# Values of two head groups made by a Strassen scheme in one early stage

## The chip, the cores and the metric

The kernel runs on one core of a Trainium2 chip. The metric is the device time of one execution in microseconds (us). The engines are TensorE (PE; its weight loads are shown as PEld), VectorE (DVE), ScalarE (ACT), GpSimd (POOL) and SyncE (SP), whose queue issues most of the DMAs. A time is compared by the median of several runs; the profile is one execution more.

## The reference

One layer of a decoder trunk on 1024 tokens of width 1024, in float32. What matters here is the first half:

```python
h = rms_norm(x, pre_mix_g[l])
proj = h @ w_in[l]
qa, ka, va, qb, kb, vb, gates = jnp.split(proj, split_at, axis=-1)
qb = apply_rope(qb.reshape(b, s, B_GROUPS, B_HEADS, B_HEAD_DIM), cos_b, sin_b)
vb = vb.reshape(b, s, B_GROUPS, B_HEADS, B_HEAD_DIM)
for g, (window, dil) in enumerate(B_PAIRS):
    o_g, lse_g = dilated_group(qb[:, :, g], kb[:, :, g], vb[:, :, g], window, dil)
```

The first attention (A) is differential attention over 4 heads. The second (B) has three groups of 4 heads of 128 columns, with dilations 1, 4 and 16. The values `vb` of groups 1 and 2 are together `h` (1024 x 1024) times 1024 columns of `w_in`. Gates, a mixing product and a convolutional MLP follow.

## The kernel before

Every float32 product is made of two parts: `split` (L140, L143) makes a high part on ACT and the remainder on DVE, and three matmuls (`mm3`, L146 to L149) take high x high, low x high and high x low. x stands transposed as `xh` and `xl`, 8 slices k of 128 rows by 1024 tokens.

*Start.* Three gates are projected first, from weights in `first`, while x arrives slice by slice (`load_x`, `split_x`; L342 and L343 split it). Their six PSUM banks are copied out (L375, L376) and stored to `gt_d` (L377). Then x is read again by rows, squared on ACT (L383) and made into `rstd`, the inverse root; `tables` computes sine and cosine of the positions on DVE (L295 to L304) and ACT (L305, L306); they are scaled by `rstd`, which is turned into a row by transposes (L394), written to `tab_d` and read back by `load_tabs`. Two more gates, the first head of A and its values follow.

*A.* Each of its heads runs eight query blocks; `interleave` mixes pieces of other projections (fills) between them, by `yield`ed sizes.

*B.* It has 12 steps (pair of heads, group, head). Each step runs four jobs of `attend_b`, with the next step's `proj_b` as filler: 96 matmuls of 512 columns. Further filler are the values of the next group, by `proj_v` (L429 to L464): each call makes 256 columns for two heads, as 8 row blocks x 8 k x 3 matmuls of 256 columns (L438 to L440), half of them in each of two steps. For group 0 they are split at once (L448, L449). For groups 1 and 2 ACT scales them by `rstd` (L453), they are stored to `v_d`, loaded back in the dilated order as `vperm` (L463) and split there. Only the step (pair 1, group 2, first head) has no other filler than the projection of q and k; the last step has gates.

*What sets the order.* The kernel's text gives each instruction a priority, earlier first, and `tc.high_priority` moves some ahead; a planner with costs of its own then orders each engine's instructions when the kernel is built, and takes one that is ready before one of higher priority that isn't. Each engine and each DMA queue then works strictly in that order. Tiles with the same tag share buffers; a tile in a reused buffer waits until the earlier one has no reader left. PSUM has eight banks: three `acc`, two `pt`, two `s`, one `o`. Weights go through six pairs of buffers `wh`, `wl`, raw data through `raw`.

## Time and profile before

| | |
|---|---|
| median of 3 runs | 1754.89 us (1754.01 to 1755.79) |
| the profiled execution | 1754.33 us |
| its span | 1752.5 us |
| mean granted PE clock | 0.994 |
| PE / PEld / DVE / ACT busy | 98% / 84% / 74% / 50% |
| matmuls and transposes | 8942 |

A row of groups shows line, engine, operation, tiles, shape, count, busy time and mean duration in ns, then the idle time before them and who ended it. A row of windows shows start and end, length, and for PE, PEld, DVE, ACT and POOL the busy time and the count, then the granted PE clock, the share of the DMA engines and GB/s. A row of the timeline shows start, duration, engine, line and tiles. A row of waits shows who waited for whom, the total, how often, and the longest. A row of DMA issues shows the count, the size of one and the median time to landing.

### The profile page before, as it was taken

How to read it: one execution, taken by the hardware profiler on the slowest of the kernel's cores; microseconds unless marked ns; L12 is line 12 of the kernel's file. 1: busy time of each engine (PE TensorE's matmuls, PEld its weight loads, DVE VectorE, ACT ScalarE, POOL GpSimd, SP SyncE). 2: the span in 40 equal slices, each digit the busy share in tenths (PEclk: the TensorE clock that was granted, in tenths of full speed). 3: DMA queues.
4: the chain of work that ended last, by engine and by line, in shares of the span. 5: the costliest groups of instructions: out<-in, count | busy, mean ns of one | idle time of the engine just before them, and what ended most of it. 6: DMA issues, size and time to landing. Idle time of an engine off the chain costs nothing.

```text
span 1752.5 us, 24382 instructions
## 1 busy us (share of the span) xinstructions
PE 1724.8 (98%) x8942; PEld 1469.5 (84%) x8942; DVE 1295.2 (74%) x2548; ACT 868.1 (50%) x1585; POOL 50.5 (3%) x78
## 2 busy tenths in 40 slices
PE   9999999999999999999999999999999999999997
PEld 7888898889988888888887888878888888878886
DVE  4766877775455566554575767899998999689978
ACT  5456564643455645465662533364444444355452
POOL 0000000000000000000000400300000000000000
PEclk9999999999999999999999999999999999999998
DMA  7510112211131234231386542123222223196624
GB/s 262 186 55 31 65 57 73 85 49 55 55 97 55 97 98 154 72 96 55 117 293 207 161 152 97 36 76 99 91 85 90 78 74 105 55 340 215 209 78 156
DMA packets 100407, 197.62 MB, mean 113 GB/s; under 512 B 16368, under 2 KB 23216, under 8 KB 100288
## 3 DMA queue, kind: packets, MB, share of 16 engines
q1 hardware_dynamic: 92192, 185.06, 32.0%
q10 hardware_dynamic: 8096, 11.01, 1.7%
q8 instruction: 70, 1.15, 0.3%
q14 instruction: 49, 0.40, 0.1%
HBM read 152.37 MB, written 43.66 MB: 112 GB/s over the span
## 4 chain that ended last, share of the span: by engine, by line
PE 77%; DVE 8%; DMA 8%; ACT 3%; issue 3%; SPq 1%; POOL 0%; DVEq 0%; ACTq 0%; POOLq 0%
PE acc L147 15%; PE acc L148 15%; PE acc L149 15%; PE acc L438 3%; PE acc L440 3%; PE acc L439 3%; PE acc L1312 2%; PE acc L1313 2%; PE acc L1311 2%; PE o L485 2%; PE pt L472 2%; PE acc L989 2%; PE acc L990 2%; PE acc L988 2%; DVE wlo L140 1%
## 5 line engine op out<-in xcount | busy, mean ns | idle before, releaser
L147 PE MATMUL acc<-xh,whi 128*128 128x512 f32 x744 | 297.3, 401 | 3.9 <-ACT xh L342 2.5
L148 PE MATMUL acc<-xh,wlo 128*128 128x512 f32 x744 | 298.2, 401 | 1.5 <-DVE wlo L140 1.5
L149 PE MATMUL acc<-xl,whi 128*128 128x512 f32 x744 | 294.7, 398 | 0.0
L143 ACT ACTIVATE whi<-raw 128x512 fp32r<-128x512 f32 (+1 forms) x258 | 158.7, 624 | 206.3 <-PE acc L149 138.5
L140 DVE TENSOR_TENSOR wlo<-raw,whi 128x512 fp32r<-128x512 f32 (+1 forms) x255 | 180.5, 716 | 57.2 <-ACT whi L143 56.4
L147 PEld LDWEIGHTS acc<-xh,whi 128*128 128x128 f32 x744 | 140.5, 189 | 34.5 <-ACT xh L342 3.7
L148 PEld LDWEIGHTS acc<-xh,wlo 128*128 128x128 f32 x744 | 140.6, 189 | 29.0 <-DVE wlo L140 1.7
L149 PEld LDWEIGHTS acc<-xl,whi 128*128 128x128 f32 x744 | 140.8, 189 | 27.5
L147 PE MATMUL acc<-mh,whi 128*128 128x512 f32 x400 | 155.7, 390 | 0.3 <-ACT mh L143 0.2
L148 PE MATMUL acc<-mh,wlo 128*128 128x512 f32 x400 | 155.6, 389 | 0.0
L149 PE MATMUL acc<-ml,whi 128*128 128x512 f32 x400 | 155.4, 389 | 0.0
L438 PE MATMUL acc<-whi,xh 128*128 128x256 f32 x512 | 147.6, 288 | 1.0 <-DVE t L421 1.0
L440 PE MATMUL acc<-wlo,xh 128*128 128x256 f32 x512 | 148.1, 289 | 0.0
L439 PE MATMUL acc<-whi,xl 128*128 128x256 f32 x512 | 147.9, 289 | 0.0
L420 ACT ACTIVATE t<-acc 64x512 f32<-64x512 f32 (+1 forms) x160 | 94.7, 592 | 39.4 <-PE acc L149 36.9
L1186 DVE TENSOR_TENSOR u<-acc,u 128x512 f32<-128x512 f32 x133 | 90.6, 685 | 26.7 <-PE acc L149 26.7
L143 ACT ACTIVATE whi<-s 128x512 fp32r<-128x512 f32 x76 | 47.0, 628 | 106.9 <-PE acc L149 97.7
L438 PEld LDWEIGHTS acc<-whi,xh 128*128 128x128 f32 x512 | 97.7, 191 | 2.0 <-DVE t L421 1.4
L439 PEld LDWEIGHTS acc<-whi,xl 128*128 128x128 f32 x512 | 97.7, 191 | 0.6
L440 PEld LDWEIGHTS acc<-wlo,xh 128*128 128x128 f32 x512 | 97.7, 191 | 0.2
L147 PEld LDWEIGHTS acc<-mh,whi 128*128 128x128 f32 x400 | 75.1, 188 | 16.3 <-ACT mh L143 0.5
L149 PEld LDWEIGHTS acc<-ml,whi 128*128 128x128 f32 x400 | 75.1, 188 | 15.7
(311 smaller groups left out, 3875.6 us busy)
## 6 DMA issues: line engine op xcount, KB each, us to landing
raw<-in_w_in SPq DMA_DIRECT2D x126, 256.0 KB, 2.8
raw<-in_w_up SPq DMA_DIRECT2D x88, 256.0 KB, 2.8
raw<-c_d SPq DMA_DIRECT2D x48, 256.0 KB, 3.6
c_d<-c SPq DMA_DIRECT2D x22, 512.0 KB, 2.6
raw<-in_w_down SPq DMA_DIRECT2D x37, 256.0 KB, 4.0
gl<-gt_d SPq DMA_DIRECT2D x16, 512.0 KB, 5.2
gt_d<-gate ACTq DMA_DIRECT2D x26, 256.0 KB, 2.1
og_d<-osb SPq DMA_DIRECT2D x12, 512.0 KB, 3.0
```

What stands on the lines that cost most here:

```text
L140: eng.tensor_tensor(lo, src, hi.bitcast(F32), op=ALU.subtract)
L143: nc.scalar.activation(hi, src, AF.Copy)
L147: nc.tensor.matmul(o, sh, mh, start=first, stop=False)
L148: nc.tensor.matmul(o, sl, mh, start=False, stop=False)
L149: nc.tensor.matmul(o, sh, ml, start=False, stop=last)
L420: nc.scalar.activation(t1[dst], ps[src], AF.Copy)
L438: nc.tensor.matmul(ps, xh[:, k, tk], wh[:, w], start=k == 0, stop=False)
L439: nc.tensor.matmul(ps, xl[:, k, tk], wh[:, w], start=False, stop=False)
L440: nc.tensor.matmul(ps, xh[:, k, tk], wl[:, w], start=False, stop=k == KC - 1)
L472: nc.tensor.transpose(ps[:, n * P : (n + 1) * P], t, ident)
L485: nc.tensor.matmul(o[:, q0 : q1 + 1], vs[b // 4][0][:, b % 4, c], t[:, part], start=first and n == part == 0, stop=False)
L1186: nc.vector.tensor_tensor(to, made(p), x, op=ALU.add)
```

## The change

The four calls of `proj_v` for groups 1 and 2 go away. In their place, right after the first three gates, one stage makes all 1024 columns at once: x and the weights are cut into 2 x 2 blocks (512 x 512 each), and seven products of blocks give the result instead of eight (Strassen's scheme in Winograd's form, the one that the MLP of this kernel has too). `sums_x` makes three of the four sums of x while x arrives, and the fourth, negated, is written over block b12 of x itself before the loop; p7's steps load that block again. A step `n` is one product and one of its four k: `fetch_v` loads weights up to 8 steps ahead, `ready_v` sums and splits them up to 5 ahead, four groups of three matmuls follow, and after the fourth k `take_v` adds the four banks into `ys_v`. Two sets of four banks alternate between the products. At step 4 the squares of x are put in, at step 18 the angles, at step 26 the first two blocks of the result are scaled and stored by ACT's queue; the tables and their reloading stand behind the stage. `values_by` is what is left of `values_of` for groups 1 and 2: loads in dilated order and a split. The first gates take the slices of x in the order 0, 4, 1, 5, 2, 6, 3, 7, and x has six buffers instead of three.

```diff
+XT_BUFS, NORM_AT, ANGLES_AT, STORE_AT = 6, 4, 18, 26
+
+K_FIRST = (0, 4, 1, 5, 2, 6, 3, 7)
...
-            order += [("v", VB + g * 512 + pair * 256, i) for i in range(2)]
+            if g == 0:
+                order += [(VB + pair * 256, i) for i in range(2)]
...
-    v_d = dram.tile([4, S, 256], F32, name="v_d")
+    v_d = dram.tile([S, 1024], F32, name="v_d")
...
+    xw0 = open_pool(st_v, "xw0", side="right")
+    t2, t3, t4 = ([xw0.tile([P, 4, 512], F32R, tag=n + p, name=n + p) for p in "hl"] for n in ("t2", "t3", "t4"))
+    tb = open_pool(st_v, "tb", side="right")
+    kq, tq = [slice(i * 4, (i + 1) * 4) for i in range(2)], halves()
+    b11, b12, b21, b22 = ([t[:, k, t_] for t in (xh, xl)] for k in kq for t_ in tq)
...
         def load_x(k, parts=1):
-            xts[k] = prep.tile([P, S], F32, tag="xt", name="xt", bufs=3)
+            xts[k] = prep.tile([P, S], F32, tag="xt", name="xt", bufs=XT_BUFS)
...
+        t1_raw = [tb.tile([P, 2, 512], F32, tag=t, name="t1") for t in ("kk", "ang")]
+
+        def sums_x(k):
+
+            low, high = xts[k], xts[k + 4]
+            g1, g2 = gpre[:, k : k + 1], gpre[:, k + 4 : k + 5]
+            e, o = (tb.tile([P, 2, 512], F32, tag=t, name=t) for t in ("sin", "cos"))
+            nt1 = t1_raw[k // 2][:, k % 2]
+
+            def plus(out, x, g, y, op):
+                nc.vector.scalar_tensor_tensor(out, x, g, y, op0=ALU.mult, op1=op)
+
+            nc.scalar.activation(e[:, 0], low[:, 512:], AF.Copy, scale=g1)
+            plus(nt1, low[:, :512], g1, e[:, 0], ALU.subtract)
+            plus(e[:, 1], high[:, 512:], g2, e[:, 0], ALU.subtract)
+            split(t3[0][:, k], t3[1][:, k], e[:, 1])
+            plus(o[:, 0], high[:, 512:], g2, nt1, ALU.add)
+            split(t2[0][:, k], t2[1][:, k], o[:, 0])
+            plus(o[:, 1], high[:, :512], g2, o[:, 0], ALU.subtract)
+            split(t4[0][:, k], t4[1][:, k], o[:, 1])
...
-        load_x(1)
-        split_x(1)
+        load_x(4)
+        split_x(4)
         load_first(256, 1024)
         split_first(256, 512)
         split_first(512, 1024)
-        for k in range(2, KC):
+        for n, k in enumerate(K_FIRST[2:], 2):
             load_x(k)
             split_x(k)
+            if n % 2:
+                sums_x(K_FIRST[n - 3])
+        sums_x(3)
...
-        for k in range(KC):
-            w = slice(k * P, (k + 1) * P)
+        for j, k in enumerate(K_FIRST):
+            w = slice(j * P, (j + 1) * P)
             for n, ps in enumerate(pss):
                 (wh, wl), sl = first[n // 2], halves()[n % 2]
-                mm3(ps, wh[:, w], wl[:, w], xh[:, k, sl], xl[:, k, sl], k == 0, k == KC - 1)
+                mm3(ps, wh[:, w], wl[:, w], xh[:, k, sl], xl[:, k, sl], j == 0, j == KC - 1)
         for n, i in enumerate(FIRST_GATES):
...
-        for m in range(8):
-            t = prep.tile([P, D], F32, tag="xt", name="xn", bufs=3)
-            dma(t, a["x"][m * P : (m + 1) * P, :])
-            sq = prep.tile([P, D], F32, tag="kk", name="sq")
-            nc.scalar.activation(sq, t, AF.Square, accum_out=ssx[:, m : m + 1])
-        with tc.high_priority(offset=60):
-            nc.vector.tensor_copy(rstd, rsqrt(ssx, D, prep, "rx"))
-            spread = rstd_row.rearrange("p (m q) -> p m q", q=P)
-            nc.vector.tensor_copy(spread, rstd.unsqueeze(2).to_broadcast([P, 8, P]))
...
+    def norm_x():
+
+        ssx = tiny.tile([P, 2, 32], F32, name="ssx", bufs=1)[:, :, :8]
+        for m in range(8):
+            for half, sl in enumerate(halves()):
+                t = load_raw(a["x"][m * P : (m + 1) * P, sl], next(tags))
+                nc.scalar.activation(t, t, AF.Square, accum_out=ssx[:, half, m : m + 1])
+        tt(ssx[:, 0], ssx[:, 0], ssx[:, 1], ALU.add)
+        nc.vector.tensor_copy(rstd, rsqrt(ssx[:, 0], D, tb, "rx"))
+
+    def make_tables(*tab):
+        nc.scalar.activation(tab[0], tab[0], AF.Sin)
+        nc.scalar.activation(tab[1], tab[1], AF.Sin, bias=half_pi)
+        spread = rstd_row.rearrange("p (m q) -> p m q", q=P)
+        nc.vector.tensor_copy(spread, rstd.unsqueeze(2).to_broadcast([P, 8, P]))
+        neg = tb.tile([P, S], F32, tag="kk", name="neg")
+        for half, sl in enumerate(halves()):
+            row = psum(F32, pt, "pt")
+            for b in range(4):
+                nc.tensor.transpose(row[:, b * P : (b + 1) * P], spread[:, half * 4 + b], ident)
+            nc.scalar.activation(rstd_row[:, sl], row, AF.Copy)
+            nc.vector.scalar_tensor_tensor(neg[:, sl], tab[0][:, sl], -1.0, row, op0=ALU.mult, op1=ALU.mult)
+            nc.vector.tensor_tensor(tab[0][:, sl], tab[0][:, sl], row, op=ALU.mult)
+            nc.vector.tensor_tensor(tab[1][:, sl], tab[1][:, sl], row, op=ALU.mult)
+        for t, to in zip((tab[1], tab[0], neg), tab_d):
+            dma(to, t)
...
+    with ExitStack() as st_y:
+        wv = open_pool(st_y, "wv")
+        yv = open_pool(st_y, "yv")
+        order_v = (("p1", b11), ("p5", b12), ("p6", t2), ("p7", t3), ("p3", b22), ("p2", b21), ("p4", t4))
+        steps_v = [(p, x, k) for p, x in order_v for k in range(4)]
+        wa, wz = ([t[:, k % 2] for t in [q.tile([P, 2, 512], F32, tag=f"{n}{i}", name=n) for i in range(2)] for k in range(2)]
+                  for n, q in (("wa", first_w), ("wz", wv)))
+        ys_v = {(q, m): yv.tile([P, 512], F32, tag=f"y{q}{m}", name="yv") for q in range(4) for m in range(4)}
+        ready, got_v = {}, {}
+        tags = itertools.cycle(("raw", "t1", "t2"))
...
+        def fetch_v(n):
+            p, _, k = steps_v[n]
+            if p == "p1":
+                dma(wa[k], w_at_v(0, 0, k))
+            which = {"p5": ((1, 0), (1, 1)), "p7": ((1, 0),), "p3": ((0, 1),), "p2": ((0, 1),), "p4": ((1, 1),)}.get(p, ())
+            got_v[n] = [load_raw(w_at_v(i, j, k), next(tags)) for i, j in which]
+
+        def ready_v(n):
+            p, _, k = steps_v[n]
+            raw = got_v.pop(n)
+            src = wa[k] if p in ("p1", "p7") else wz[k] if p in ("p5", "p6", "p3") else raw[0]
+            if p == "p5":
+                tt(src, *raw, ALU.add)
+            if p == "p6":
+                tt(src, src, wa[k])
+            if p == "p7":
+                tt(src, src, raw[0])
+            if p == "p3":
+                tt(src, raw[0], src)
+            ready[n] = slot_w()
+            split(*ready[n], src)
+
+        def take_v(p, m, ps):
+
+            c11, c12, c21, c22 = (ys_v[q, m] for q in range(4))
+            if p == "p1":
+                nc.scalar.activation(c11, ps, AF.Copy)
+            if p == "p5":
+                nc.scalar.activation(c22, ps, AF.Copy)
+            if p == "p6":
+                tt(c21, ps, c11, ALU.add)
+                tt(c12, c21, c22, ALU.add)
+            if p == "p7":
+                tt(c21, ps, c21, ALU.add)
+                tt(c22, c21, c22, ALU.add)
+            if p in ("p3", "p2", "p4"):
+                to = {"p3": c12, "p2": c11, "p4": c21}[p]
+                tt(to, ps, to, ALU.add)
+
+        def store_v(q, i, j):
+
+            for m in range(4):
+                y, tk = ys_v[q, m], j * 4 + m
+                nc.scalar.activation(y, y, AF.Copy, scale=rstd[:, tk : tk + 1])
+                nc.scalar.dma_start(v_d[tk * P : (tk + 1) * P, i * 512 : (i + 1) * 512], y)
+
+
+        for k in range(4):
+            nt1 = t1_raw[k // 2][:, k % 2]
+            nc.scalar.activation(b12[0][:, k], nt1, AF.Copy, scale=-1.0)
+            nc.vector.scalar_tensor_tensor(b12[1][:, k], nt1, -1.0, f32(b12[0][:, k]), op0=ALU.mult, op1=ALU.subtract)
+
+        fetched = made = 0
+        for n, (p, x, k) in enumerate(steps_v):
+            while fetched < min(n + 8, len(steps_v)):
+                fetch_v(fetched)
+                fetched += 1
+            while made < min(n + 5, len(steps_v)):
+                ready_v(made)
+                made += 1
+            if k == 0:
+                banks = ([psum() for _ in range(3)] + [psum(F32, ps_o, "o")] if n // 4 % 2 == 0 else
+                         [psum(F32, q, t) for q, t in ((ps_s, "s"), (pt, "pt")) for _ in range(2)])
+            if n == NORM_AT:
+                norm_x()
+            if n == ANGLES_AT:
+                pos = [load_raw(a["positions"][sl].partition_broadcast(P), next(tags)) for sl in halves()]
+                args = [tb.tile([P, S], F32, tag=n, name=n) for n in ("sin", "cos")]
+                angles(pos, *args, tb)
+            if n == STORE_AT:
+                store_v(3, 1, 1)
+                store_v(1, 0, 1)
+            wh, wl = ready.pop(n)
+            for m in range(4):
+                tk = slice(m * P, (m + 1) * P)
+                mm3(banks[m], x[0][:, k, tk], x[1][:, k, tk], wh, wl, k == 0, k == 3)
+            if k == 3:
+                for m in range(4):
+                    take_v(p, m, banks[m])
+            if p == "p7":
+
+                raw = load_raw(a["xT"][k][:, 512:], next(tags))
+                nc.scalar.activation(xh[:, k, 512:], raw, AF.Copy, scale=gpre[:, k : k + 1])
+                nc.vector.scalar_tensor_tensor(xl[:, k, 512:], raw, gpre[:, k : k + 1], f32(xh[:, k, 512:]), op0=ALU.mult,
+                                               op1=ALU.subtract)
+        store_v(0, 0, 0)
+        store_v(2, 1, 0)
+        make_tables(*args)
+    st_v.close()
+    tabs = open_pool(attn, "tabs", side="right")
+    cos_a, sin_a = load_tabs(64, 32)
+    slots = open_pool(attn, "slots", side="right")
...
+    def values_by(dil, c, res):
+
+        n = S // dil // P
+        src = v_d[:, c : c + 256].rearrange("(ih p r) c -> p r ih c", r=dil, ih=n)
+        for i in range(2):
+            v = slot("vperm", (P, 4, 256), F32)
+            for ih in range(n):
+                dma(v.rearrange("p (r ih) c -> p r ih c", ih=n)[:, :, ih], src[:, i * 4 // n : (i + 1) * 4 // n, ih])
+            h, l = v_tiles()
+            split(h, l, v)
+            res.append((h, l))
+            yield 0
...
-        if h % 2 == 0 and n + 2 < len(steps):
+        if h % 2 and nxt[1]:
+            fills.insert(0, (values_of(*nxt[:2]), 0))
+        elif h % 2:
+            fills.append((ahead, 4))
+        elif n + 2 < len(steps) and steps[n + 2][1] == 0:
             ahead = values_of(*steps[n + 2][:2])
             fills.append((itertools.islice(ahead, 8), 4))
-        elif h % 2:
-            fills.append((ahead, 4))
```

More of the change, by code (lines that the diff above doesn't have):

```diff
@@ L287, in new_tabs, with angles @@
         return [tabs.tile([P, S], F32, tag=t, name=t) for t in ("cos", "sin")]
-    def tables(sin, cos, tmp):
-        pos = tmp.tile([P, S], I32, tag="kk", name="pos")
+    def angles(pos, sin_of, cos_of, tmp):
         ang = tmp.tile([P, S], F32, tag="ang", name="ang")
         kk = tmp.tile([P, S], F32, tag="kk", name="kk")
-        dma(pos, a["positions"].partition_broadcast(P))
-        nc.vector.tensor_copy(ang, pos)
+        for sl, p in zip(halves(), pos):
+            nc.vector.tensor_copy(ang[:, sl], p.bitcast(I32))
         nc.vector.tensor_scalar(ang, ang, cols[:, 0:1], None, op0=ALU.mult)
-        for dst, off in ((sin, 0.0), (cos, 0.25)):
+        for dst, off in ((sin_of, 0.0), (cos_of, 0.25)):
             nc.vector.tensor_scalar(kk, ang, 1.0 / (2 * math.pi), off, op0=ALU.mult, op1=ALU.add)
@@ L426, in v_tiles @@
-    def v_tiles(i):
-        return [slot(t, (P, 4, 256)) for t in ("vh", "vl")]
-    def proj_v(col, res, wk=None, via=None, dil=1, ms=range(8)):
-        us = [load_unit(w_in[where[("v", col, i)]]) for i in range(2)]
+    def norm_x():
[6 more added lines that the diff above has]
+        nc.vector.tensor_copy(rstd, rsqrt(ssx[:, 0], D, tb, "rx"))
@@ L432, in proj_v @@
+    st_v.close()
+    tabs = open_pool(attn, "tabs", side="right")
+    cos_a, sin_a = load_tabs(64, 32)
+    slots = open_pool(attn, "slots", side="right")
+    def proj_v(col, res, ms=range(8)):
+        us = [load_unit(w_in[where[col, i]]) for i in range(2)]
         for m in ms:
@@ new lines, in rotated @@
+    def rotated(ps, cos, sin, sl, quarter):
+        t1 = rt.tile([P, 512], F32, tag="t1", name="t1")
+        t2 = rt.tile([P, 512], F32, tag="t2", name="t2")
+        for q in range(P // quarter):
+            src, dst = slice((q ^ 1) * quarter, ((q ^ 1) + 1) * quarter), slice(q * quarter, (q + 1) * quarter)
+            nc.scalar.activation(t1[dst], ps[src], AF.Copy)
+        nc.vector.tensor_tensor(t2, ps, cos[:, sl], op=ALU.mult)
+        nc.vector.tensor_tensor(t1, t1, sin[:, sl], op=ALU.mult)
+        nc.vector.tensor_tensor(t2, t2, t1, op=ALU.add)
+        return t2
@@ L468, in turned, with v_tiles @@
+    def v_tiles():
+        return [slot(t, (P, 4, 256)) for t in ("vh", "vl")]
     def turned(blocks, pool, bufs):
@@ L1442, in layout @@
     w = f["w_in"][0]
+    arr["w_v"] = w[:, VB + 512 : VB + 1536].reshape(KC, P, 1024)
     us = []
-    for u in plan():
-        if u[0] == "t":
-            us.append(units(w[:, u[1] : u[1] + P], KC, P))
-        else:
-            us.append(units(w[u[2] * 512 : (u[2] + 1) * 512, u[1] : u[1] + 256], 4, 256))
+    for n, c in enumerate(plan()):
+        if isinstance(c, tuple):
+            us.append(units(w[c[1] * 512 : (c[1] + 1) * 512, c[0] : c[0] + 256], 4, 256))
+            continue
+        blocks = w.reshape(KC, P, -1)[list(K_FIRST) if n < len(FIRST_GATES) else range(KC), :, c : c + P]
+        us.append(units(blocks.reshape(D, P), KC, P))
     arr["w_in"] = np.stack(us)
```

112 lines of the change are left out of this document (36 added, 76 removed).

## The prediction

> **What bounds the kernel now.** I read the page first, then who waited for whom on TensorE (PE), then the timeline of matmuls, then the windows.
>
> ```profile
> span 1752.5 us, 24382 instructions
> PE 1724.8 (98%) x8942; PEld 1469.5 (84%) x8942; DVE 1295.2 (74%) x2548; ACT 868.1 (50%) x1585; POOL 50.5 (3%) x78
> ```
>
> PE is busy for 98% of the span. That alone could hide waits, because a busy PE row runs from each matmul's issue to its modelled end. The list of PE's waits settles it:
>
> ```profile
> engine line waited for: us in total, times, longest us
> PE acc L148 <- DVE wlo L140: 2.8, 2, 1.5
> PE acc L147 <- ACT xh L342: 2.5, 2, 1.7
> PE acc L147 <- DVE ya L926: 1.3, 1, 1.3
> ...
> PE acc L438 <- DVE t L421: 1.0, 1, 1.0
> ```
>
> The longest entries add up to a few microseconds of 1752.5. So PE's own work is the bound nearly everywhere, and a change is worth what it takes off PE, less any wait that it makes there. The price of a matmul is not its duration but the distance from its start to the next start:
>
> ```profile
> 105.73 0.28 PE L438 MATMUL acc<-whi,xh 128*128 128x256 f32 x1
> ...
> 108.97 0.28 PE L438 MATMUL acc<-whi,xh 128*128 128x256 f32 x1
> ```
>
> ```profile
> 177.40 0.40 PE L148 MATMUL acc<-xh,wlo 128*128 128x512 f32 x1
> ...
> 179.67 0.39 PE L149 MATMUL acc<-xl,whi 128*128 128x512 f32 x1
> ```
>
> In the first run 27 steps take 108.97 - 105.73 = 3.24 us, so 0.120 us per 256-wide matmul of values. In the second 10 steps take 2.27 us, so 0.227 us per 512-wide matmul.
>
> **The change part by part.** *Removed from PE:* four calls of `proj_v` (two pairs of heads, groups 1 and 2), each 8 row blocks x 8 k x 3 = 192 matmuls, in all 768 of 256 columns: 768 x 0.120 = 92.2 us. *Added:* seven products, each 4 k x 4 row blocks x 3 = 48 matmuls of 512 columns, in all 336: 336 x 0.227 = 76.3 us. PE's work falls by 15.9 us.
>
> In a sentence by itself: the Trainium skill ("TensorE: Matmul & The Clock Gate", section "Back-to-back issue gap") gives N / 2.4 + 2.5 ns for a warm matmul, which is 109 and 216 ns, and by it the fall would be 83.7 - 72.6 = 11.1 us and the time 4.8 us more than mine. The trace's 120 and 227 ns are both longer than the page's, the narrow ones by more, and the trace decides.
>
> The price of the removed ones has two ends. The low one is half a 512-wide matmul, 0.1135 x 768 = 87.2 us. The high one comes from a step of the second attention with values between its matmuls against the one step that has none:
>
> ```profile
> 805.10:846.00 40.90, 40.90 (x260) 36.32 (x258) 20.69 (x46) 23.66 (x47) 0.00 (x0) 1.00 0.18 61
> 846.00:877.20 31.20, 31.20 (x165) 26.12 (x164) 19.89 (x53) 22.06 (x43) 0.00 (x0) 1.00 0.46 143
> ```
>
> The groups of the two windows show 97 and 113 512-wide matmuls:
>
> ```profile
> L147 PE MATMUL acc<-xh,whi 128*128 128x512 f32 x33 | 13.4, 409 | 0.0
> L438 PE MATMUL acc<-whi,xh 128*128 128x256 f32 x32 | 9.3, 290 | 0.0
> ...
> L147 PE MATMUL acc<-xh,whi 128*128 128x512 f32 x38 | 15.4, 405 | 0.0
> ```
>
> With 16 matmuls x 0.227 = 3.6 us taken off the second, the difference is 40.9 - 27.6 = 13.3 us a step, over 8 steps 106 us; part of it is a heavier attention group. I take 92.2: it is the clean spacing, and nearer to the low end. The fall in PE work is then between 10.9 and 30 us.
>
> *The first gates.* Four calls of `sums_x` go in front of the product stage: each has 4 copies and splits on ScalarE (ACT) and 7 operations on VectorE (DVE), 28 x 0.69 = 19.3 us of DVE and 16 x 0.63 = 10 us of ACT, by these rows:
>
> ```profile
> L140 DVE TENSOR_TENSOR wlo<-raw,whi 128x512 fp32r<-128x512 f32 x251 | 177.6, 715 | 53.8 <-ACT whi L143 53.0
> L396 DVE SCALAR_TENSOR_TENSOR neg<-sin,pt 128x512 f32<-128x512 f32 x2 | 1.3, 680 | 0.0
> L143 ACT ACTIVATE whi<-raw 128x512 fp32r<-128x512 f32 x252 | 156.6, 629 | 204.4 <-PE acc L149 138.5 <-issue 17.9 <-PE acc L1312 15.3
> ```
>
> ```profile
> 0.00:10.00 10.00, 6.23 (x15) 4.26 (x16) 3.00 (x6) 4.26 (x7) 1.43 (x7) 0.99 0.70 221
> 10.00:20.00 10.00, 10.00 (x39) 8.08 (x38) 8.20 (x13) 7.13 (x11) 2.67 (x2) 0.84 0.90 320
> 20.00:30.00 10.00, 10.00 (x46) 8.29 (x45) 6.21 (x6) 5.78 (x8) 0.00 (x0) 1.00 0.78 235
> 30.00:40.00 10.00, 10.00 (x46) 8.29 (x45) 0.69 (x1) 4.93 (x9) 0.00 (x0) 1.00 0.83 267
> ```
>
> DVE worked 18.1 of these 40 us and has 15 to 16 us free after the first operands arrive. It needs 19.3, so it comes out 2 to 4 us late when the first gates end at about 44 us. Behind it queue the copies that free two of the gates' banks, the negated sums written over the fourth part of x, and the first weight splits of p1; PE waits for the last. I take 2 us (0 to 6). The reads of x that move away (8 squares on ACT) leave room for the added ACT work.
>
> *The stage.* PE needs 76.3 us. DVE gets 28 splits, 16 sums of weights, 28 takes, 4 negated sums, 4 restorations of x: 80 x 0.69 = 55 us; then 16 operations of the angles, the inverse root, and `make_tables`' 7:
>
> ```profile
> L302 DVE SCALAR_TENSOR_TENSOR sin<-kk,sin 128x1024 f32<-128x1024 f32 x1 | 1.2, 1226 | 0.0
> L298 DVE TENSOR_SCALAR kk<-ang 128x1024 f32<-128x1024 f32 x2 | 1.4, 686 | 0.0
> L168 DVE TENSOR_TENSOR rxw<-rxw,rxv 128x8 f32<-128x8 f32 x3 | 0.5, 166 | 0.1
> ```
>
> Six at 1.22, six at 0.69, the scaling and two casts are 13 us; the root about 2.3; the tables 7 x 0.69 = 4.8. In all some 75 us by durations. ACT gets 28 splits, 16 squares, 8 takes, 8 copies for x, 16 scalings: 76 x 0.63 = 48 us, plus two sines and the issue of 16 stores, also within it. The stage's DVE load just fits under its own 76.3 us and runs into the two gates behind (2 x 48 x 0.227 = 21.8 us of PE), which cover the tables: sines, transposes, three stores of tables and their reloading finish before the first head's projection takes its cosines. Without that cover the chain of store and reload would stand open, about 6 us. What remains is a lump: the angles' 13 us stand in front of the takes of p3, whose four banks p4 needs. I take 2 us for it (0 to 8). The two sets of four banks make the other takes free. The stores of v go out on ACT's queue as before, 16 of them, and the late reads are wanted hundreds of microseconds later.
>
> *The second attention* loses 11.5 us of PE filler in 8 of its steps. I cost that at nothing: in the window 846.0 to 877.2 above, a step with only the next head's projections as filler, PE is busy 31.20 of 31.20 us.
>
> *Sum:* 1754.33 - 92.2 + 76.3 + 4 = 1742.4 us for the profiled execution, which stood 0.56 us under the median 1754.89: **1743 us**.
>
> **Rivals.** *More gain.* The values cost 13.3 us a step, as the two windows compare, and DVE never holds PE: -106.4 + 76.3, 1725 us at the end of the bounds; with the usual 4 us, 1729. For it: short matmuls spoil their neighbours' spacing. Against it: the clean run.
>
> *VectorE decides in the stage's second half.* What happens when DVE has no pause is in the old tables:
>
> ```profile
> 50.00:60.00 10.00, 10.00 (x50) 8.38 (x49) 8.74 (x13) 2.33 (x5) 0.00 (x0) 1.00 0.42 153
> 60.00:70.00 10.00, 9.57 (x42) 7.60 (x42) 9.96 (x15) 3.50 (x4) 0.00 (x0) 1.00 0.48 174
> ```
>
> At 8.74 of 10 PE loses nothing, at 9.96 it loses 0.43. If the backlog of the first gates and the angles both come in full, 6 + 8 = 14 us less the 4 already in the sum: 1753 at most, 1749 in the middle.
>
> *Operands come too late, no change.* Weights, 16 halves of x and the reloads share six raw buffers on SyncE's in-order queue, and the first weight sums write where a gate's output waits for its store:
>
> ```profile
> raw<-in_w_in SPq DMA_DIRECT2D x126, 256.0 KB, 2.8
> gt_d<-gate SPq DMA_DIRECT2D x3, 512.0 KB, 4.6
> ```
>
> About 72 transfers of 256 KB, 18.9 MB, belong to the stage, 12 to 18 of them fetched ahead; the other 15 MB in 76.3 us are 200 GB/s. The rows above reached 235 to 320 in the first gates. At 174 GB/s, the row of 60 to 70 us, they would take 86 us, so 10 us of waits on top of 4, with two spells of half clock behind them:
>
> ```profile
> 172.59 0.63 PE L148 MATMUL acc<-xh,wlo 128*128 128x512 f32 x1
> 173.02 0.63 PE L149 MATMUL acc<-xl,whi 128*128 128x512 f32 x1
> ```
>
> After waits of about 2 us in all, matmuls stood 0.43 us apart instead of 0.227 for 11 of them: 2.2 us. That gives 1743 + 10 + 2 = 1755, no change. Beside the row: the Trainium skill (same page, section "What's actually happening") lets the clock fall only after an idle window of about 3.4 us; by that rule short waits would cost only themselves and this rival 1753, while the row shows the fall after less.
>
> *The second attention starves, slower.* In the eight steps without values PE has about 29.4 us of work, DVE up to this:
>
> ```profile
> 638.70:680.00 41.30, 38.89 (x242) 34.29 (x241) 26.15 (x67) 19.59 (x47) 0.00 (x0) 1.00 0.51 151
> ```
>
> Less the 1.4 us of its value splits, 24.7 of 29.4 us, 84%, where the step that ran without filler had 64%; and in that window PE already lost 2.4 us. If each of the eight steps waits 3 us, 24 us come back: 1767 us. It decides from 15.9 - 4 = 11.9 us on, 1.5 us a step. Against it: 8.74 of 10 was harmless above.
>
> **How the numbers follow.** Chances: the forecast 0.52 (its own range 1737 to 1748), more gain 0.10, VectorE in the stage 0.18, late operands 0.08, starving 0.12. A measurement of this kernel tells about 0.2%, 3.5 us, from no change. Faster is the first three, 0.80; same 0.08; slower 0.12. The range 1732 to 1758 leaves out the starving steps and the far half of more gain, 0.17 together.
>
> **What would show it.** Right: no matmul of 256 columns on the removed values' groups, 336 more of 512 at 0.227 us apart in a stretch of 76 to 80 us from about 44 us on; PE's list of waits longer by under 6 us; steps of the second attention 29 to 31 us apart with PE full. Wrong: DVE at 9.9 of 10 with PE under 9.5 in the stage; PE waits on raw transfers there; spells of half clock; PE waiting for DVE or ACT in the second attention, steps 32 us or more apart.

## The result and the profile after

The changed kernel takes 1742.42 us (median of 4, 1740.99 to 1743.06) beside 1754.45 for the kernel before (4 runs): a ratio of 0.9933, 95% interval 0.9915 to 0.995. The forecast was 1743. A second set of runs on another chip (below) gave 0.9914 (0.99 to 0.9928). The total was right; the parts of the sum were not all right, and two of them made up for each other.

The page of the changed kernel begins so:

```profile
span 1740.3 us, 23773 instructions
...
PE 1709.9 (98%) x8510; PEld 1445.5 (83%) x8510; DVE 1350.6 (78%) x2642; ACT 886.3 (51%) x1629; POOL 54.4 (3%) x78
```

PE's busy time falls by 14.9 us, the span by 12.2. Where they went is read from five stretches that end at the same places in both kernels: the first narrow matmul of values, the second attention's first scores, its last scores, the first matmul of the mixing product, the end. First the kernel before, then the changed one:

```profile
0.00:88.50 88.50, 84.23 (x354) 68.09 (x355) 52.90 (x85) 46.08 (x72) 4.93 (x11) 0.98 0.68 222
88.50:425.40 336.90, 332.99 (x1987) 294.76 (x1987) 251.19 (x696) 188.33 (x374) 1.62 (x4) 0.99 0.18 58
425.40:899.60 474.20, 471.43 (x2893) 417.00 (x2893) 267.64 (x618) 259.50 (x544) 0.00 (x0) 1.00 0.31 99
899.60:1002.20 102.60, 101.23 (x456) 83.35 (x456) 66.50 (x103) 49.49 (x72) 17.65 (x14) 1.00 0.64 208
1002.20:1752.50 750.30, 734.97 (x3257) 606.31 (x3255) 657.03 (x1048) 324.69 (x524) 26.34 (x50) 0.99 0.35 120
```

```profile
0.00:167.90 167.90, 161.85 (x691) 132.71 (x692) 120.74 (x197) 92.28 (x165) 9.32 (x11) 0.98 0.57 192
167.90:504.60 336.70, 332.84 (x1987) 294.74 (x1986) 249.21 (x694) 187.71 (x372) 0.00 (x0) 0.99 0.18 58
504.60:883.70 379.10, 378.16 (x2126) 327.00 (x2125) 252.54 (x597) 230.60 (x493) 1.14 (x4) 1.00 0.30 99
883.70:992.20 108.50, 104.19 (x456) 85.74 (x455) 72.42 (x111) 51.27 (x76) 17.82 (x14) 0.97 0.62 207
992.20:1740.30 748.10, 732.90 (x3257) 605.27 (x3255) 655.68 (x1046) 324.49 (x523) 26.13 (x49) 1.00 0.35 120
```

| stretch | before | after | difference | in the sum |
|---|---|---|---|---|
| to the first narrow matmul of values | 88.5 | 167.9 | +79.4 | +76.3 + 2 + 2 |
| to the second attention's first scores | 336.9 | 336.7 | -0.2 | 0 |
| to its last scores | 474.2 | 379.1 | -95.1 | -92.2 |
| to the mixing product | 102.6 | 108.5 | +5.9 | 0 |
| to the end | 750.3 | 748.1 | -2.2 | 0 |
| all | 1752.5 | 1740.3 | -12.2 | -11.9 |

The matmul counts are those of the change, but for a record or two at the borders: 337 more in the first stretch, 767 fewer in the third (the sum has 336 and 768). In the stage PE lost nothing: its 336 matmuls start between 43.25 and 119.18 us, 75.9 us without a gap. This is the changed kernel in ten-microsecond windows:

```profile
30.00:40.00 10.00, 10.00 (x46) 8.29 (x45) 10.00 (x18) 3.97 (x8) 0.00 (x0) 1.00 0.00 1
...
80.00:90.00 10.00, 10.00 (x46) 8.28 (x45) 10.00 (x21) 4.05 (x7) 2.50 (x2) 1.00 0.36 119
...
120.00:130.00 10.00, 7.76 (x30) 6.22 (x28) 8.08 (x14) 5.71 (x9) 0.00 (x0) 0.83 0.55 190
```

PE (the second figure) is at 10.00 even where DVE (the fourth) is at 10.00 too, and falls only in the last row, right behind the stage. The spacing within the stage is the forecast's; 12 steps take 102.41 - 99.69 = 2.72 us, 0.227 us each:

```profile
99.69 0.39 PE L154 MATMUL pt<-whi,xh 128*128 128x512 f32 x1
...
102.41 0.39 PE L154 MATMUL pt<-whi,xh 128*128 128x512 f32 x1
```

From the list of PE's waits over the whole execution:

```profile
PE acc L154 <- DVE ya L1076: 2.5, 1, 2.5
PE acc L154 <- DVE yv L299: 2.2, 1, 2.2
...
PE o L634 <- ACT osb L919: 1.8, 1, 1.8
```

The rows with `yv` and `osb` are new, the one with `ya` had 1.3 us. `yv` is the wait behind the stage, for a take of p4. DVE's timeline there:

```profile
118.20 0.69 DVE L147 TENSOR_TENSOR wlo<-raw,whi 128x512 fp32r<-128x512 f32 x1
118.81 1.22 DVE L320 SCALAR_TENSOR_TENSOR cos<-kk,cos 128x1024 f32<-128x1024 f32 x1
121.26 0.69 DVE L147 TENSOR_TENSOR wlo<-raw,whi 128x512 fp32r<-128x512 f32 x1 [1.23 <-ACT whi L150]
121.87 0.68 DVE L299 TENSOR_TENSOR yv<-acc,yv 128x512 f32<-128x512 f32 x1
```

p4's last matmul had been issued before 120 us, but the take (L299) that frees its bank stood in DVE's order behind the cosine's arithmetic and behind a split of the next gate's weights, which itself waited 1.23 us.

Of the second attention's steps, a short one and a long one:

```profile
771.20:800.00 28.80, 28.80 (x160) 24.78 (x160) 18.69 (x44) 17.86 (x40) 0.00 (x0) 1.00 0.21 68
599.50:635.40 35.90, 35.90 (x191) 30.56 (x191) 26.35 (x53) 25.79 (x49) 0.00 (x0) 1.00 0.22 71
```

PE is full in both. Neither has a matmul of values (those of group 0 lie at 655 to 669 and 697 to 710 us); the longer one has 125 matmuls of 512 columns where the shorter has 94, so the projections are not spread evenly over the steps. The loss comes after the steps, between the last scores and the mixing product. There DVE stood waiting for the loads of the merge of the groups' outputs (`og`); first the kernel before, then the changed one, from 865 to 1003 us:

```profile
DVE og L841 <- DMA og<-og_d: 8.3, 2, 5.0
...
DVE og L841 <- DMA raw<-in_w_mix_out: 4.5, 1, 4.5
```

```profile
DVE og L989 <- DMA og<-og_d: 19.1, 4, 6.5
```

12.8 us became 19.1, and what is queued behind on DVE (gates, gated products `ya`) came late for PE. Most of the difference is the first of the four merges, which waits 5.6 us now and had not waited before. The timelines show how, first before, then after:

```profile
876.54 0.67 ACT L771 ACTIVATE osb<-o 128x256 f32<-128x256 f32 x1
...
890.58 1.75 DVE L841 TENSOR_TENSOR og<-og,mw 128x1536 f32<-128x1536 f32 x1
```

```profile
867.62 1.06 ACT L150 ACTIVATE oah<-ot 128x1024 fp32r<-128x1024 f32 x1 [4.89 <-DMA ot<-oa_d]
...
869.90 0.65 ACT L919 ACTIVATE osb<-o 128x256 f32<-128x256 f32 x1
...
882.67 1.76 DVE L989 TENSOR_TENSOR og<-og,mw 128x1536 f32<-128x1536 f32 x1 [5.59 <-DMA og<-og_d]
```

The copy of the last output that this merge needs (`osb`) now stands on ACT behind a split (`oah`) that waits 4.89 us for its load; before, the planner had put it in front of such a wait. The output is stored at 870.58 us, and the merge's load goes out when that store has landed, at 875.49. The same order, with 4.4 to 5.6 us of waiting, is in every trace of a kernel with the stage whose steps and merges are those of the changed kernel. This is read from traces; no run moves the copy alone.

### The profile page after: what moved, and what is told of

Read it like the earlier page. It is cut to its first block, busy times and chain, and to the rows that moved or that the text cites. A ratio compares the mean times of both kernels' runs of the same rounds, so it can differ in the third digit from the quotient of the medians.

```text
span 1740.3 us, 23773 instructions
## 1 busy us (share of the span) xinstructions
PE 1709.9 (98%) x8510; PEld 1445.5 (83%) x8510; DVE 1350.6 (78%) x2642; ACT 886.3 (51%) x1629; POOL 54.4 (3%) x78
## 4 chain that ended last, share of the span: by engine, by line
PE 82%; DVE 7%; DMA 6%; ACT 2%; issue 2%; SPq 1%; POOL 0%; DVEq 0%; ACTq 0%; POOLq 0%
PE acc L155 16%; PE acc L154 16%; PE acc L156 16%; PE acc L1460 3%; PE acc L1459 3%; PE acc L1458 3%; PE o L634 2%; DMA og<-og_d 2%; PE pt L621 2%; PE acc L1139 2%; PE acc L1140 2%; PE acc L1138 2%; PE acc L578 2%; PE acc L577 2%; PE acc L579 2%
## 5 line engine op out<-in xcount | busy, mean ns | idle before, releaser
L150 ACT ACTIVATE whi<-raw 128x512 fp32r<-128x512 f32 (+1 forms) x250 | 153.9, 624 | 226.3 <-PE acc L156 145.5
L147 DVE TENSOR_TENSOR wlo<-raw,whi 128x512 fp32r<-128x512 f32 (+1 forms) x247 | 174.7, 714 | 50.2 <-ACT whi L150 49.2
L156 PEld LDWEIGHTS acc<-xl,whi 128*128 128x128 f32 x744 | 141.5, 190 | 27.7
L609 DVE TENSOR_TENSOR t<-acc,cos 128x512 f32<-128x512 f32 x64 | 44.1, 689 | 65.5 <-ACT t L608 63.2
L155 PEld LDWEIGHTS acc<-mh,wlo 128*128 128x128 f32 x400 | 75.1, 188 | 15.6
L1459 PE MATMUL acc<-whi,wlo 128*128 128x512 f32 x220 | 77.3, 389 | 0.0
L1458 PE MATMUL acc<-whi 128*128 128x512 f32 x220 | 75.8, 389 | 0.0
L578 PE MATMUL acc<-whi,xl 128*128 128x256 f32 x256 | 73.6, 288 | 0.0
L579 PE MATMUL acc<-wlo,xh 128*128 128x256 f32 x256 | 73.5, 287 | 0.0
```

Source lines behind the costliest of these rows:

```text
L147: eng.tensor_tensor(lo, src, hi.bitcast(F32), op=ALU.subtract)
L150: nc.scalar.activation(hi, src, AF.Copy)
L155: nc.tensor.matmul(o, sl, mh, start=False, stop=False)
L156: nc.tensor.matmul(o, sh, ml, start=False, stop=last)
L578: nc.tensor.matmul(ps, xl[:, k, tk], wh[:, w], start=False, stop=False)
L579: nc.tensor.matmul(ps, xh[:, k, tk], wl[:, w], start=False, stop=k == KC - 1)
```

## The experiments

Each ran beside the kernel before, on the same chip. Since chips and executions differ by a few microseconds, a run is judged by its ratio to the kernel before; the changed kernel stands at 0.9933 and 0.9914, and 0.001 is 1.75 us.

### One product twice

In p2 each matmul is done and added twice, so that the values hold p2 twice: 48 more matmuls.

```diff
-                mm3(banks[m], x[0][:, k, tk], x[1][:, k, tk], wh, wl, k == 0, k == 3)
+                for again in range(2 if p == "p2" else 1):
+                    mm3(..., k == again == 0, k == 3 and (p != "p2" or again == 1))
```

> The product p2 is computed and added twice, so 48 more 512-wide matmuls stand in the stage and nothing else does (the first 512 columns of values for the first half of the tokens then hold p2 twice). Theory 'TensorE work is the currency': 48 x 0.227 = 10.9 us come back in full, 1753.3 us, 0.6240% above the changed kernel. Rival 'VectorE or the operands set the stage's length': the added matmuls fill TensorE time that was spent waiting, so less than 4 us, below 1746.5 us.

1743.86 us, ratio 0.9951 (0.9937 to 0.9965): 3.1 to 6.5 us more than the changed kernel for 10.9 us of matmuls. By the numbers on record the theory that TensorE's work is paid one for one fell. The trace says where the rest went. First the changed kernel, then this one: the first narrow matmul of values comes 6.0 us later,

```profile
167.88 0.28 PE L577 MATMUL acc<-whi,xh 128*128 128x256 f32 x1
```

```profile
120.00:130.00 10.00, 10.00 (x48) 8.31 (x47) 4.70 (x8) 4.14 (x8) 0.00 (x0) 1.00 0.48 165
...
173.87 0.28 PE L578 MATMUL acc<-whi,xh 128*128 128x256 f32 x1
```

and the wait and the half clock at 120 to 130 us are gone: PE is at 10.00 there and not at 7.76, the clock at 1.00 and not 0.83. Those are 2.2 us and half of a 3.4 us spell, 3.9 us. Longer p2 gave DVE the time to be through with the angles before p4 ended. The stage itself is longer by exactly what was added: from its first matmul to its last it takes 86.81 us here and 75.93 in the changed kernel, 10.9 more. The rest of the difference is that it starts 0.8 us earlier here (42.42 and not 43.25 us).

### The stage without Strassen's scheme

The stage makes the same columns in eight block products, without any sums, 384 matmuls; takes are copies.

```diff
-        order_v = (("p1", b11), ("p5", b12), ("p6", t2), ("p7", t3), ("p3", b22), ("p2", b21), ("p4", t4))
-        steps_v = [(p, x, k) for p, x in order_v for k in range(4)]
+        steps_v = [(i, j, k) for i in range(2) for j in range(2) for k in range(8)]
...
-            if n % 2:
-                sums_x(K_FIRST[n - 3])
-        sums_x(3)
...
```

> The same stage without Strassen's scheme: eight block products (384 matmuls of 512 columns instead of 336), no sums of x, no sums of weights, results copied out by ScalarE and scaled and stored as in the change. Theory 'TensorE work is the currency': 384 x 0.227 = 87.2 us instead of 76.3, so 10.9 us more than the changed kernel, 1753 us; 5 us under the kernel before if the wait behind the stage stays away, the same as it if that wait stays. Rival 'the gain comes from gathering the values in one stage with wide matmuls, not from the scheme': 1742 to 1746 us.

1744.96 us, ratio 0.9962 (0.9948 to 0.9975). By the number the rival is met (1742 to 1746): against the two ratios of the changed kernel the scheme is worth 5.1 to 8.4 us, and not the 10.9 of its 48 matmuls. The trace shows both parts. The stage takes 86.81 us, 10.9 more, so the matmuls are worth what the theory says; but the plain stage has no wait behind it, so the 3.9 us of that wait come off: 10.9 - 3.9 = 7.0. In this trace the first narrow matmul of values is only 3.8 us later than in the changed kernel, since the stage also starts 3.0 us earlier (40.2 us). By the same prices, gathering the values in wide matmuls without the scheme is worth 92.2 - 384 x 0.227 = 5.0 us.

### More work for VectorE in the second attention

The low parts of q and k are subtracted twice over; nothing else changes.

```diff
-                nc.vector.tensor_tensor(l, t, o.bitcast(F32), op=ALU.subtract)
+                for _ in range(2):
+                    nc.vector.tensor_tensor(l, t, o.bitcast(F32), op=ALU.subtract)
```

> Each evacuation of a projection of q or k for the second attention does its last VectorE subtraction twice (the same result), 0.98 us each, 4 per step, 12 steps, 47 us of VectorE in all; TensorE work unchanged. Theory 'TensorE sets the steps of the second attention, VectorE has a quarter of its time free there': up to 6 us more, below 1749 us. Rival 'with the filler gone VectorE is the bound of these steps': at least half of the added work of the eight steps, 16 us or more, above 1758 us.

1749.21 us, ratio 0.9981 (0.9969 to 0.9992), 8.4 to 11.7 us more: neither number on record was met. The stretches of this run, first the steps, then the one up to the mixing product:

```profile
502.10:886.80 384.70, 380.96 (x2126) 327.47 (x2125) 290.33 (x641) 233.87 (x498) 1.14 (x4) 1.00 0.28 95
886.80:999.60 112.80, 105.61 (x456) 86.59 (x455) 71.97 (x109) 49.92 (x73) 18.14 (x14) 0.95 0.61 206
```

DVE has 37.8 us more in the steps, and they take 5.6 us longer (PE idles 3.74 of them instead of 0.94); the stretch behind takes 4.3 more. So the steps of the changed kernel have room on DVE, but not for everything: 9.9 us of some 47 added in all, about a fifth, came through in these two stretches. The rival that the second attention starves needs far more work there than the change leaves.

### The gates' weights earlier

The two gates behind the stage take their raw weights through six buffers and not two.

```diff
+    raw_tags = [itertools.repeat("raw")]
...
-            raw = load_raw(src[:, sl])
+            raw = load_raw(src[:, sl], next(raw_tags[0]))
...
+        raw_tags[0] = itertools.cycle(("raw", "t1", "t2"))
...
```

> The weights of the two gates behind the stage are loaded through all six raw buffers instead of two. Theory 'the wait of 2.24 us at 120 us comes from VectorE's queue standing behind a weight split whose load is late': the wait and the spell of half clock behind it (3.4 us at half speed, 1.7 us) go away, 3 to 4 us less, 1738.5 us. Rival 'VectorE is late there because of the angles and tables themselves': no change within 1 us, 1742 us.

1741.76 us, ratio 0.9941 (0.9926 to 0.9956), no gain. The wait for the take went, another came 5 us later, for weights of the next gate:

```profile
PE acc L155 <- ACT whi L151: 7.2, 1, 7.2
```

The number is the rival's, the vanished wait the theory's. In this trace DVE has the cosine done at 116.3 us and no split stands between it and the takes, so the run doesn't part late weights from the angles.

### The changed kernel again, and one product four times

The next four ran on one chip. The changed kernel itself first:

> The changed kernel itself, beside the next three, so that they are compared on one chip. All theories: within 2 us of 1742.4.

1736.43 us, ratio 0.9914 (0.99 to 0.9928). All theories had 2 us around 1742.4; it came 6 lower, the kernel before 2.8 lower. Its trace has the same instructions, the same wait behind the stage and the same order at the second attention's end, where it takes 2.1 us less:

```profile
883.70:990.10 106.40, 102.02 (x455) 83.20 (x454) 71.65 (x110) 51.33 (x76) 18.13 (x14) 1.00 0.63 212
```

The granted clock is 1.00 in this stretch; in the first profile it was 0.97, which is two spells of half clock of 3.4 us. PE's busy time, 104.19 us there and 102.02 here, shows what they cost: 2.2 us. The spans of the two profiles, 1740.3 and 1736.6 us, differ by 3.7.

Then p2 four times over, 144 matmuls more than in the changed kernel, the diff of the first experiment with 4 in place of 2:

> The product p2 is computed and added four times (144 more 512-column matmuls, 32.6 us by the row of 227 ns; values wrong). In the run with it twice, 6.0 of the 10.9 us added came through by the first values of the first attention, 4.9 being a wait and a spell of half clock behind the stage that went away. Theory A (TensorE's work in the stage is paid one for one, and only that one wait was saved): the first narrow values matmul 27.7 us later than in the changed kernel, the end 23 to 28 us later, 1765 to 1770 us. Theory B (the stage or what follows it has slack that takes up TensorE's work): under 20 us later, below 1762.

1764.94 us, ratio 1.0078 (1.0063 to 1.0092), 28.5 us over the changed kernel on the same chip, just beside theory A's numbers (1765 to 1770 us, 23 to 28 us later) and far from theory B's: TensorE's work is paid one for one once the wait is gone. The first narrow matmul of values here:

```profile
194.55 0.28 PE L578 MATMUL acc<-whi,xh 128*128 128x256 f32 x1
```

That is 194.55 - 173.87 = 20.7 us behind the run with p2 twice, for 96 matmuls x 0.227 = 21.8. The stage takes 108.57 us against 86.81, which is 21.8; it starts 1.1 us earlier here (41.34 and not 42.42 us). The first 10.9 us had cost 6.0. Theory A's 27.7 us over the changed kernel are 26.0 here, against its trace beside this run (168.58 us).

### The stores earlier

```diff
-            if n == STORE_AT:
+            if n == 18:
                 store_v(3, 1, 1)
+            if n == 22:
                 store_v(1, 0, 1)
+            if n == 26:
+                store_v(0, 0, 0)
...
-        store_v(0, 0, 0)
         store_v(2, 1, 0)
```

> Three of the four quadrants are scaled and stored as soon as they are done (steps 18, 22 and 26) and not all at the end of the stage, so that the weights of the gate behind the stage do not land behind 4 MB of stores. If the 2.2 us wait of TensorE at 122.7 us and the half clock after it come from the late weights: both go, the first narrow values matmul starts 3.5 to 4.5 us earlier, and 1738 to 1740 us. If the wait is put in its place by VectorE's order alone: no change, 1742.

1736.59 us, ratio 0.9913 (0.99 to 0.9926), no change, and the wait stays. PE's one wait at this place is 3.0 us, for the take. DVE's order in front of it:

```profile
116.98 1.22 DVE L320 SCALAR_TENSOR_TENSOR cos<-kk,cos 128x1024 f32<-128x1024 f32 x1
118.81 0.69 DVE L147 TENSOR_TENSOR wlo<-raw,whi 128x512 fp32r<-128x512 f32 x1 [0.62 <-ACT whi L150]
```

The theory of late weights fell: the split in front of the take now waits 0.62 us instead of 1.23, and PE waits no less. It is the order on DVE.

### The merges on GpSimd

```diff
-            nc.vector.tensor_tensor(og, og, wt, op=ALU.mult)
...
+            eng = nc.vector if to is None else nc.gpsimd
+            eng.tensor_tensor(og, og, wt, op=ALU.mult)
...
-                split(to[0][h][:, sl], to[1][h][:, sl], og[:, 0])
+                later(2, lambda: split(to[0][h][:, sl], to[1][h][:, sl], t[:, sl]))
...
-        later(2 * i + 3, fn)
+        later(2 * i + 2, fn)
```

> The three operations that merge the groups' outputs of the last two heads of the second attention run on GpSimd and not on VectorE, the splits behind them come two jobs later, the last head's merge is begun one product earlier. If what was given back at the end of the second attention (8 us between its last scores and the second branch) comes from VectorE standing in order behind loads of the outputs (19.1 us in four waits): TensorE's waits for VectorE at 884 and 925 us and the half clock after them go, 4 to 8 us less, 1734 to 1738 us. If other work is late instead (GpSimd's own operations, the splits): 1741 to 1746 us.

1738.86 us, ratio 0.9931 (0.9918 to 0.9944), between the two numbers expected. The median is 2.4 us above that of the changed kernel beside it, and the intervals overlap. The wait was handed on. From 883 to 990 us GpSimd waits for the loads, ScalarE for GpSimd, VectorE for ScalarE:

```profile
POOL og L990 <- DMA mw<-e_d: 16.5, 1, 16.5
ACT obh L150 <- POOL ot L996: 14.2, 1, 14.2
DVE obl L147 <- ACT obh L150: 13.7, 2, 8.1
```

This run says nothing on the cause, since VectorE stood in order behind the same loads as before, two engines removed; the last experiment settles it.

### The stage's sums left out

```diff
-            if n % 2:
-                sums_x(K_FIRST[n - 3])
-        sums_x(3)
...
-        order_v = (("p1", b11), ("p5", b12), ("p6", t2), ("p7", t3), ("p3", b22), ("p2", b21), ("p4", t4))
+        order_v = (("p1", b11), ("p5", b12), ("p6", b21), ("p7", b22), ("p3", b22), ("p2", b21), ("p4", b11))
...
-            if p == "p6":
-                tt(src, src, wa[k])
...
```

> Strassen's matmuls, takes and loads stay, the sums and splits of the activations and three of the four sums of the weights are left out (values wrong), which takes some 30 us of work from VectorE, most of it in the first 45 us. Theory (the sums lie behind TensorE's work, as the sum of the prediction has them but for 2 us at the first product): the end 0 to 3 us earlier than the changed kernel's ratio of 0.9914 gives, 0.990 to 0.9915. Rival (VectorE's sums hold the stage or its start back): 4 us or more earlier, a ratio under 0.9890.

1740.04 us, ratio 0.9929 (0.9911 to 0.9946). VectorE's busy time up to the first narrow matmul of values fell from 120.7 to 94.3 us, and nothing got faster. The ratio lies above what either side expected; its interval reaches the theory's range and stays clear of the rival's, which fell. The wait for the take behind the stage is still there (2.4 us), since the angles are.

### The angles earlier

```diff
-XT_BUFS, NORM_AT, ANGLES_AT, STORE_AT = 6, 4, 18, 26
+XT_BUFS, NORM_AT, ANGLES_AT, STORE_AT = 6, 4, 10, 26
```

> The angles of the tables are worked out from the eleventh step of the stage on and not from the nineteenth, so that the cosine's four operations of 1.2 us are no longer on VectorE between the last split and the takes of p4. Theory (the wait of TensorE of 2.2 to 3.0 us behind the stage is the angles' lump, one product later than the prediction put it): the wait goes or falls under 1 us, with it 1 to 4 us: ratio 0.9890 to 0.9908. Rival (the wait is for the gate's weights in front of the takes): the wait stays over 1.5 us and the ratio within 0.9908 to 0.9920.

The wait is gone. VectorE's order now, and the window behind the stage:

```profile
114.41 1.24 DVE L320 SCALAR_TENSOR_TENSOR cos<-kk,cos 128x1024 f32<-128x1024 f32 x1
...
116.15 0.70 DVE L322 TENSOR_SCALAR cos<-cos 128x1024 f32<-128x1024 f32 x1
116.75 1.90 DVE L299 TENSOR_TENSOR yv<-acc,yv 128x512 f32<-128x512 f32 x3
```

```profile
120.00:130.00 10.00, 10.00 (x46) 8.27 (x45) 5.35 (x9) 8.20 (x14) 0.00 (x0) 1.00 1.01 363
```

The cosine is done before the takes and PE is full. So the wait was the angles, together with the split behind them. The time: 1736.59 us, ratio 0.9908 (0.9892 to 0.9923), at the edge of what was expected. Against 0.9914 that is 1 us, less than the intervals can tell, so the 3.9 us are shown in the trace and not in the medians.

### A third of the stage's matmuls

Each product keeps only its high x high matmul, so that the values are less exact: 112 instead of 336, with all other work left.

```diff
-                mm3(banks[m], x[0][:, k, tk], x[1][:, k, tk], wh, wl, k == 0, k == 3)
+                nc.tensor.matmul(banks[m], x[0][:, k, tk], wh, start=k == 0, stop=k == 3)
```

> Each of the stage's products keeps one of its three matmuls (112 instead of 336, values wrong), 50.7 us less of TensorE, with all of VectorE's, ScalarE's and the queues' work left. Theory (TensorE's work alone sets the stage, VectorE's 51 us of 76 lie behind it): the stage gets shorter until VectorE or the loads decide, so by 15 to 35 us, with TensorE's waits filling the rest: 1701 to 1721 us. If nothing but TensorE had a part: 50 us, 1686. If VectorE were already near its limit in the changed kernel: under 8 us, above 1728.

1730.16 us, ratio 0.987 (0.9855 to 0.9886): only 7.7 to 11 us faster, for 50.7 us less of TensorE. The 15 to 35 us expected were not met; by the number the reading that VectorE is near its limit (above 1728 us) was. The trace says where the time went. PE's waits from 44 to 130 us and two windows:

```profile
PE s L550 <- ACT whi L150: 13.5, 4, 6.9
PE acc L550 <- ACT whi L150: 6.9, 7, 2.0
PE acc L154 <- DVE gate L231: 5.9, 1, 5.9
```

```profile
90.00:100.00 10.00, 5.80 (x18) 3.38 (x16) 10.00 (x20) 1.89 (x3) 0.00 (x0) 0.84 0.30 94
...
120.00:130.00 10.00, 4.13 (x15) 3.05 (x14) 4.69 (x8) 7.05 (x12) 0.00 (x0) 0.77 0.97 349
```

The stage's last matmul starts at 97 us and not at 120, so the other engines and the loads need about 53 us for what TensorE takes 76 to do. VectorE is not near its limit in the changed kernel. Whether it or the loads set the 53 us is open: PE's waits are for ACT's splits of the weights (`whi`), and in the same window ACT waits 7.1 us for loads of the stage's weights. Of these 23 us 11.3 are left at the first narrow matmul of values (157.3 us against 168.6 in the second trace of the changed kernel); the rest is lost right behind the stage, by a wait of 5.9 us for a gate's evacuation and by half clock (0.84 and 0.77 in the rows). So the stage has some 23 us of cover, of which matmuls saved in it brought half in this run.

### The last two heads' merges left out

Neither the groups' outputs nor their weights are loaded for heads 2 and 3, VectorE's three operations are gone, and the splits read a resident tile in place of the merged outputs.

```diff
         def load(half):
+            if to is not None:
+                return
...
+            if to is not None:
+                split(to[0][h][:, sl], to[1][h][:, sl], rstd_row[:, sl])
+                return
```

> The merges of the last two heads are left out: neither the groups' outputs nor their weights are loaded, VectorE's three operations per half are gone, and the splits take a resident tile in their place (values wrong); the small work on the groups' sums stays. In all kernels with the stage, 105 to 109 us lie between the last scores' start in the second attention and the first of the mixing matmuls, 102.6 in the kernel before. Theory (the 3 to 6 us given back there come from VectorE standing in order behind the merge's loads): this stretch falls to 102 us or less, TensorE's waits for VectorE's gated products in it (3.1 us in the changed kernel's second profile) to under 1 us, and the ratio to 0.987 to 0.9895. Rival (other work is late there: the gates' tiles, the weights, the half clock): the stretch stays at 104 us or more, the ratio at 0.9905 to 0.992.

1729.38 us, ratio 0.9875 (0.9856 to 0.9894). The stretch from the last scores to the mixing product:

```profile
883.60:984.10 100.50, 100.50 (x456) 83.51 (x454) 61.90 (x99) 49.84 (x73) 19.34 (x16) 1.00 0.52 179
```

PE is busy for 100.50 of 100.50 us, where it was 104.19 of 108.50 and 102.02 of 106.40. The theory held: the merges hold PE back here, by 5.9 us in the second profile of the changed kernel, by 8.0 in the first (half clock included), and by 2.1 in the kernel before. As loads and arithmetic were left out together, the run doesn't part them; DVE at 72 of 108 us speaks for the waits.

This run and the one with a third of the matmuls leave out work that the result needs. Of the runs that do all of it, none beats the changed kernel by more than the intervals; the one with the angles earlier comes nearest.

## Why the prediction was right, step by step

*The bound.* Right. PE's work is what the time is paid in: the stage gets 21.8 us longer for the 21.8 us between two and four times p2.

*The removed matmuls, 92.2 us.* The second attention's steps got 95.1 us shorter. PE's idle time there fell from 2.77 to 0.94 us, which is 1.8 of the 2.9 more; the other 1.1 stay open. The clean spacing of 0.120 us was the right end to choose, the comparison of two windows (106) was not.

*The added matmuls, 76.3 us.* Right, 0.227 us apart without a gap. (The 216 ns that the Trainium skill, "TensorE: Matmul & The Clock Gate", section "Back-to-back issue gap", gives for this width were too short here too.) Neither the rival of more gain (106 us for the removed matmuls) nor that of late operands (10 us of waits in the stage) came true.

*The first gates, 2 us.* Wrong, it is nothing. VectorE was full from 20 to 40 us as the step had it, but PE has no wait at the hand-over. p1's first weights are not queued behind the sums: the planner put their split ahead of the last slice's, at 41.40 us as this row of VectorE's timeline shows. Leaving the sums out gained nothing: the stage starts at 40.0 to 43.8 us in the eleven traces that have them and at 40.2 and 44.9 in the two that don't.

```profile
41.40 0.69 DVE L147 TENSOR_TENSOR wlo<-wa,whi 128x512 fp32r<-128x512 f32 x1
```

*The angles' lump, 2 us.* The mechanism was right, the place one product late, the size too small: not p3's takes but p4's stand behind the cosine, PE waits 2.2 us, and half clock adds 1.7, 3.9 for the 2 (of 0 to 8). With the angles earlier both go.

*The stage's cover.* Its VectorE load, "some 75 us by durations", is right as a sum of durations, but it is not what VectorE needs within the stage: the windows from 40 to 120 us show it busy for 65 of 80 us, since operations of 0.69 us start 0.60 us apart and the tables come behind the stage. With a third of the matmuls the stage takes 53 us. The rival that VectorE decides in the stage did not come about.

*The second attention, nothing.* PE is full in the steps as forecast, but their length was no sign: those without values are 28.8 to 35.9 us long and not 29 to 31, some past the 32 us that was to show the forecast wrong, because the projections are spread unevenly. The step that failed is that the account ended with the steps: the merges behind them gave 5.9 us back in this profile (3.8 in the other). Their instructions were no part of the change, but the planner put them in another order with it, as the timelines above show. What the argument from PE's busy share in one window missed, too, is that the last step and the branch after it have DMA waits in VectorE's order that stood close to PE already, 1.3 us of them in the row of `ya` quoted in the prediction. The rival of starving, 1.5 us a step, did not come about; the loss sits at one place.

*The total.* +3.1 for +4 in the first stretch (nothing for the first gates, the rest behind the stage), 2.9 more from the steps, 5.9 given back, and 2.2 less in the last stretch, where the profile of before had a granted clock of 0.99 and the one after 1.00. So 1742.42 for 1743 is right by its large terms and, in the last 6 us, by errors that cancel, which is luck. The start of the stage alone differs by up to 3.8 us between traces whose text is the same up to there, so a match of the first stretch within 1 us is partly luck too.

## What to carry to other kernels

Price a moved product by the start-to-start distance of its matmuls; that carried the forecast to within 1 us in the stage and 3 in the steps. Then look at the ends of each changed stretch: a stall is found not where an engine is fullest but where one instruction that frees a PSUM bank stands in order behind a lump of other work or behind a load. And a gain of a few microseconds that one profile shows can be less than what two executions of the same kernel differ by; count what left the trace, and don't claim it from the medians.

## What the runs showed of the hardware

The spells of half clock come in whole multiples of 3.41 us, but for the last, which runs past the kernel's end, and start on a fixed grid of that width: in each of 14 traces all spells begin a whole number of 3.413 us after the first one (122.638 - 9.998 = 33.00 x 3.413 in the changed kernel). A spell follows a grid interval in which PE was little busy. Of the changed kernel, the interval with the wait behind the stage and the one after it:

```profile
119.20:122.60 3.40, 1.25 (x10) 0.93 (x8) 2.17 (x4) 0.65 (x2) 0.00 (x0) 1.00 0.27 91
122.60:126.00 3.40, 3.30 (x8) 2.69 (x9) 3.40 (x6) 3.40 (x6) 0.00 (x0) 0.51 0.43 154
```

PE was busy for 1.25 of 3.40 us, 37%, and then half clock for one interval. Over the 14 traces, with the interval's busy share worked out from the matmuls' starts and ends, every interval below 44% was followed by half clock, and of those at full clock none above 70%; between them it went either way. So a wait of 2 to 3 us costs 1.7 us more or not, depending on where it falls in the grid: the changed kernel's wait of 2.2 to 2.5 us cost it in both profiles, the 3.0 us wait of the run with earlier stores did not. The Trainium skill ("TensorE: Matmul & The Clock Gate", section "What's actually happening") has the window: 3413 ns, free-running. These traces agree with both, and show besides that the window need not be idle, as the prediction had read it.
